# The digits for the one-hot rows in a PSUM bank taken from the scores' ring

## The chip, the cores and the metric

The kernel runs on one core of a Trainium2 chip. The metric is the device time of one execution in microseconds; lower is better. The times of three runs of the kernel before are shown, and one execution was profiled.

## The reference, cut to what matters

Two blocks of a network (a gated delta rule layer, a stick-breaking attention layer, then a layer of windowed attention and mLSTM) run on 512 tokens of width 1024. The change lies in the last part, `peer_ffn`, which picks 16 of 16384 experts for each token and head:

```python
q = (xb @ w_query).reshape(t, PEER_HEADS, 2, PEER_KEY_DIM // 2)
s = jnp.einsum('thpd,hpkd->thpk', q, sub_keys).astype(jnp.float32)
top_s, top_i = lax.top_k(s, K)
...
cand_i = (top_i[:, :, 0, :, None] * N_KEYS + top_i[:, :, 1, None, :]).reshape(t, PEER_HEADS, K * K)
best_s, best_pos = lax.top_k(cand_s, K)
idx = jnp.take_along_axis(cand_i, best_pos, axis=-1)
gate = jax.nn.softmax(best_s, axis=-1)
u = expert_down[idx]
act = jax.nn.gelu(jnp.einsum('td,thkd->thk', xb, u).astype(jnp.float32), approximate=False)
vv = expert_up[idx]
return jnp.einsum('thk,thkd->td', (gate * act).astype(xb.dtype), vv)
```

An expert's index has two digits below 128.

## The kernel before, in words

Weights are split into a high and a low part (`split`, lines 99 and 102: ACT rounds, then POOL or DVE subtracts) and each product is three matmuls (`mm3`, lines 106 to 108). In the last part (`peer`, from line 1217 on) three of the four blocks of 128 tokens are *dense*, the first is *sparse*.

- **Fills.** For each of 128 first digits j, `activations` loads 128 experts (`downr`, 512 KB), splits them (`downh`, `downl`), multiplies them with the tokens of the three dense blocks in 24 matmuls of 384 columns (tile `pj`), and writes the activations `w` to a DRAM buffer `wait`. A quarter of the subtractions runs on DVE (`SPL`), the rest on POOL. With each fill 1.25 rows of experts are fetched for the sparse block by an indirect DMA that POOL issues (`gdown`, line 1428), and DVE multiplies such a row with `xn`, which lies in PSUM (line 1438).
- **Picks.** `peer_pick` (line 1315) handles one block: scores in four groups of four heads and one half each (line 1326, PSUM tile `s`, a ring of two banks), copied by ACT to `sc` (line 1328, two buffers), scanned on DVE by `top16` (lines 1309 to 1313, five scans a head), then the candidates, the softmax and the two digits (`part`). A fill's worth of work is put between groups and heads.
- **Gate matrices.** `gate_matrix` (line 1384) makes for a dense block a 128 x 128 matrix per token: gates summed at the pair of digits. Three transposes put digit 1, digit 2 and gate of each of 128 slots on the partitions (`slots`). In steps of 8 tokens, 16 a block and 48 in all, DVE makes `one` (line 1402: does the counter 0 to 127 equal digit 1) and `hot` (line 1405: the same for digit 2), POOL multiplies `hot` by the gate (`two`, line 1407), PE multiplies `one` by `two` for each token (line 1412, tile `m`, a ring of two banks), ACT copies the result to `stage` (line 1413), and a DMA writes it to DRAM. With each step stand 1.33 fills.
- **Combine.** From about 2310 us on the second table is read, and PE sums over all experts (line 1504).

For these comparisons the counter stands in SBUF twice: `iota` (fp32, 128 columns) for `one`, `iota8` (bf16, 1024 columns, each value eight times) for `hot`, with digit 2 cast to bf16 (`slotsb`, line 1395).

PSUM has eight banks; in this part `xn` takes two, the projections' ring `pj` two, `s` two and `m` two. `SPARE_P` (line 328) names the banks that the first four query projections use: pj, pj, s, s.

The order on each engine is set by a scheduler from the written order and its own costs and waits; every engine works its instructions off in that order. So the order moves where a buffer or the kind of an operation changes.

Of the kernel before, what the change touches and what calls it, by code (L numbers as in the profile page):

```python
# [14 lines left out]
BF16 = mybir.dt.bfloat16  # L15
AF = mybir.ActivationFunctionType
ALU = mybir.AluOpType
AX = mybir.AxisListType

P = 128  # L20
# [304 lines left out]


class Gdn(Net):
    SPARE_SB, SPARE_2, SPARE_P = "pj pj l l", "pj pj l l", "pj pj s s"
    RAW, SB_, PART = 3, 3, 2
    FIRST, OFF, A0, WB, SPARE_0, SQ = (0, 8, 16), (), 12, 6, "v0", 8  # L330
    SP = 5
# [876 lines left out]
class Peer(Second):  # L1208
# [8 lines left out]
    def peer(self, x, out, dense, sparse):  # L1217
# [4 lines left out]
        nc, tc, a = self.nc, self.tc, self.a  # L1222
# [4 lines left out]
        with ExitStack() as st:  # L1227
            self.ring(2, 3, *self.S3)
            c = st.enter_context(tc.tile_pool(name="p_c", bufs=1))
            dram = st.enter_context(tc.tile_pool(name="p_dram", bufs=1, space=bass.MemoryType.DRAM))  # L1230
            sx = ExitStack()
            xn = sx.enter_context(tc.tile_pool(name="p_xn", bufs=1, space=bass.MemoryType.PSUM)).tile([P, D], F32, name="xn")
            s1 = ExitStack()
            self.psum(s1, s=2, m=2)
            keys = c.tile([P, NH, P], F32, name="keys")
            nc.sync.dma_start(keys, a["sub_keysT"])
            iota = c.tile([P, P], F32, name="iota")
# [1 line left out]
            small = c.tile([P, self.K], BF16, name="small")  # L1239
            nc.gpsimd.tensor_copy(small, iota[:, :self.K])  # L1240

            iota8 = c.tile([P, P, 8], BF16, name="iota8")
            nc.gpsimd.tensor_copy(iota8, iota.unsqueeze(2).to_broadcast([P, P, 8]))
            nH, nL = c.tile([P, KC, T], F32R, name="nH"), c.tile([P, KC, T], F32R, name="nL")
            self.gp = st.enter_context(tc.tile_pool(name="p_g", bufs=self.LAG + 2))
            qT = s1.enter_context(tc.tile_pool(name="p_q", bufs=1)).tile([P, NH, T], F32, name="pqT")
# [15 lines left out]
            wk = s1.enter_context(tc.tile_pool(name="p_wk", bufs=1))  # L1262
# [4 lines left out]
            def fill(share):  # L1267
                self.share += share
                while self.filled < min(P, int(self.share * P + 1e-6)):
                    j = self.filled  # L1270
                    self.dve += self.SPL
                    by_dve = self.dve >= 1
                    w, l = self.activations(j, N, nc.vector if by_dve else nc.gpsimd)
                    nc.sync.dma_start(wait[j], w)
                    self.due += self.RATE_1 if self.gs else 0.0
                    if by_dve:
                        self.dve -= 1
                    self.gather(min(int(self.due), sum(g[0] == "down" for g in self.gs)), None if by_dve else l, l if by_dve else None)
                    self.due -= int(self.due)
                    self.filled += 1  # L1280
            self.fill = fill
            gate, d1, d2 = self.peer_pick(wk, i0, qT, keys, small)
# [8 lines left out]
            G = []  # L1291
            for i in dense:
                gate, d1, d2 = self.peer_pick(wk, i, qT, keys, small)
                G.append(self.gate_matrix(wk, dram, i, gate, d1, d2, iota, iota8))
            fill(1.0)
            self.gather(sum(g[0] == "down" for g in self.gs))
            while self.came:
# [83 lines left out]
            part.append(o.rearrange("p h k -> p (h k)"))  # L1381
        return gate.rearrange("p h k -> p (h k)"), part[0], part[1]

    def gate_matrix(self, wk, dram, i, gate, d1, d2, iota, iota8):

        nc = self.nc
        TG = self.TG
        Gd = dram.tile([P // TG, P, P, TG], F32, name=f"G{i}")
        p = self.pg("s")
        for z, s in enumerate((d1, d2, gate)):  # L1390
            nc.tensor.transpose(p[:, z * P:(z + 1) * P], s, self.ident)
        sl = wk.tile([P, 3, P], F32, tag="slots", name=f"slots{i}", bufs=2)
        nc.scalar.copy(sl, p[:, :3 * P].rearrange("p (z t) -> p z t", z=3))
        slb = wk.tile([P, P], BF16, tag="slotsb", name=f"slotsb{i}", bufs=2)
        nc.scalar.copy(slb, p[:, P:2 * P])
        for tg in range(P // TG):
            stage = wk.tile([P, P, TG], F32, tag="stage", name=f"stage{i}_{tg}", bufs=2)
            for t8 in range(0, TG, 8):
                self.fill(self.BUILD / 16)
                tt = slice(tg * TG + t8, tg * TG + t8 + 8)  # L1400
                one = wk.tile([P, 8, P], F32, tag="one", name=f"one{i}_{tg}_{t8}", bufs=2)
                nc.vector.tensor_tensor(one, iota.unsqueeze(1).to_broadcast([P, 8, P]),
                                        sl[:, 0, tt].unsqueeze(2).to_broadcast([P, 8, P]), op=ALU.is_equal)
                hot = wk.tile([P, P, 8], BF16, tag="hot2", name=f"hot{i}_{tg}_{t8}", bufs=2)
                nc.vector.tensor_tensor(hot, iota8, slb[:, tt].unsqueeze(1).to_broadcast([P, P, 8]), op=ALU.is_equal)
                two = wk.tile([P, 8, P], F32, tag="two", name=f"two{i}_{tg}_{t8}", bufs=2)
                nc.gpsimd.tensor_tensor(two, hot.rearrange("p j t -> p t j"),
                                        sl[:, 2, tt].unsqueeze(2).to_broadcast([P, 8, P]), op=ALU.mult)
                for t4 in range(0, 8, 4):
                    pm = self.pg("m")  # L1410
                    for t in range(4):
                        nc.tensor.matmul(pm[:, t * P:(t + 1) * P], one[:, t4 + t], two[:, t4 + t], start=True, stop=True)
                    nc.scalar.copy(stage[:, :, t8 + t4:t8 + t4 + 4], pm.rearrange("p (t j) -> p j t", t=4))
            nc.sync.dma_start(Gd[tg], stage)
        return Gd
# [224 lines left out]
```

## Time and profile before

| | us |
|---|---|
| median of 3 runs (2845.3 to 2853.7) | 2853.34 |
| the profiled execution | 2852.8 |
| its span | 2851.0 |

The profile gives for each engine what it did when, and for idle time the instruction that ended it. PE is TensorE, PEld its weight loads, DVE is VectorE, ACT ScalarE, POOL GpSimd; "L1402" is line 1402 of the kernel before. A name before "<-" is written, those behind it are read. PEclk is the share of TensorE's full clock that was granted. A wait is put down to whatever ended it last.

### The profile page before, as it was taken

To read this page: it belongs to the slowest core of one execution; us is meant where nothing else is said; L and a number is where in the kernel's file an instruction comes from. 1 tells how busy PE (TensorE), PEld (TensorE's weight loads), DVE (VectorE), ACT (ScalarE), POOL (GpSimd) and SP (SyncE) were. 2 spreads that over 40 slices of the span, in tenths; PEclk is the share of its full clock that TensorE was granted. 3 is DMA by queue.
4 is the path that set the end of the run, shared out by engine and by line. 5 is a ranking of instruction groups with operands and counts; after the bars stand their busy time and mean duration, and the time that the engine had idled before them with its cause. 6 is when DMAs were issued, how large, how long until landed. Compare 5 with 4: busy or idle time off the path is not lost. (4 is left out here: it accounts for less than half of the span.)

```text
span 2851.0 us, 40457 instructions
## 1 busy us (share of the span) xinstructions
PE 2671.3 (94%) x14601; PEld 2266.0 (79%) x14601; DVE 1786.9 (63%) x3095; ACT 1210.9 (42%) x2508; POOL 1765.5 (62%) x1335
## 2 busy tenths in 40 slices
PE   6999898799998999999998989998998999999999
PEld 4877777697776877778786988898998978877777
DVE  7767664614446654122332989899899166778886
ACT  5566663636654454233333333333333333333332
POOL 4889883533333522433463468788788378888786
PEclk9999999899998999999999999999999999999999
DMA  6334331221011111221222587887987879999996
GB/s 240 108 119 125 111 113 31 76 90 60 31 39 54 56 45 60 74 69 66 69 79 89 160 296 261 284 290 256 314 277 281 276 272 344 340 333 331 333 328 227
DMA packets 206793, 499.35 MB, mean 175 GB/s; under 512 B 18304, under 2 KB 106624, under 8 KB 203520
## 3 DMA queue, kind: packets, MB, share of 16 engines
q1 hardware_dynamic: 167856, 359.19, 37.6%
q0 software_dynamic: 36864, 134.23, 13.1%
q10 hardware_dynamic: 1872, 3.33, 0.4%
q8 instruction: 115, 1.88, 0.3%
q14 instruction: 86, 0.70, 0.1%
HBM read 444.26 MB, written 52.43 MB: 174 GB/s over the span
## 5 line engine op out<-in xcount | busy, mean ns | idle before, releaser
L102 POOL TENSOR_TENSOR wl<-wr,wh 128x256 fp32r<-128x256 f32 (+2 forms) x499 | 414.8, 850 | 499.2 <-ACT wh L99 468.5
L102 POOL TENSOR_TENSOR upl<-upr,uph 128x1024 fp32r<-128x1024 f32 x128 | 312.9, 2445 | 97.0 <-ACT uph L99 96.3
L99 ACT ACTIVATE wh<-wr 128x256 fp32r<-128x256 f32 (+2 forms) x556 | 228.7, 445 | 302.6 <-PE pj L107 120.4
L106 PE MATMUL pj<-nH,downh 128*128 128x384 f32 x1024 | 354.3, 346 | 2.3 <-ACT w L1459 1.7
L108 PE MATMUL pj<-nH,downl 128*128 128x384 f32 x1024 | 349.6, 341 | 4.6 <-DVE downl L102 4.6
L107 PE MATMUL pj<-nL,downh 128*128 128x384 f32 x1024 | 348.8, 341 | 0.0
L102 POOL TENSOR_TENSOR downl<-downr,downh 128x1024 fp32r<-128x1024 f32 x96 | 243.9, 2542 | 129.3 <-ACT downh L99 126.4
L1504 PE MATMUL acc<-uph,wwh 128*128 128x512 f32 x768 | 302.7, 399 | 6.9 <-ACT wwh L99 6.9
L1504 PE MATMUL acc<-upl,wwh 128*128 128x512 f32 x768 | 305.4, 398 | 0.0
L99 ACT ACTIVATE downh<-downr 128x1024 fp32r<-128x1024 f32 x128 | 135.4, 1059 | 307.0 <-PE pj L107 163.2
L102 DVE TENSOR_TENSOR wwl<-wo,wwh 128x384 fp32r<-128x384 f32 x128 | 196.1, 1533 | 76.4 <-ACT wwh L99 70.5
L1504 PE MATMUL acc<-uph,wwl 128*128 128x512 f32 x768 | 232.4, 398 | 6.6 <-DVE wwl L102 6.5
L108 PE MATMUL pj<-hH,wl 128*128 128x512 f32 x544 | 222.8, 411 | 0.9 <-POOL wl L102 0.8
L106 PE MATMUL pj<-hH,wh 128*128 128x512 f32 x544 | 220.5, 405 | 2.1 <-ACT mo L1175 1.1
L107 PE MATMUL pj<-hL,wh 128*128 128x512 f32 x544 | 215.8, 397 | 0.0
L99 ACT ACTIVATE uph<-upr 128x1024 fp32r<-128x1024 f32 x128 | 134.8, 1053 | 174.9 <-POOL upl L102 116.1
L106 PEld LDWEIGHTS pj<-nH,downh 128*128 128x128 f32 x1024 | 193.7, 189 | 6.6 <-ACT w L1459 2.0
L108 PEld LDWEIGHTS pj<-nH,downl 128*128 128x128 f32 x1024 | 193.3, 189 | 5.3 <-DVE downl L102 4.9
L107 PEld LDWEIGHTS pj<-nL,downh 128*128 128x128 f32 x1024 | 193.6, 189 | 0.0
L1428 POOL DMA_INDIRECT gdown<-in_peer_down,idx x128 | 165.7, 1295 | 44.3 <-issue 13.7
L1504 PEld LDWEIGHTS acc<-uph,wwh 128*128 128x128 f32 x768 | 145.6, 190 | 44.6 <-ACT wwh L99 9.4
L1504 PEld LDWEIGHTS acc<-uph,wwl 128*128 128x128 f32 x768 | 144.8, 189 | 43.4 <-DVE wwl L102 8.3
(621 smaller groups left out, 6702.2 us busy)
## 6 DMA issues: line engine op xcount, KB each, us to landing
downr<-in_peer_down_j SPq DMA_DIRECT2D x128, 512.0 KB, 4.8
upr<-in_peer_up_j SPq DMA_DIRECT2D x128, 512.0 KB, 6.3
wr<-in_w_in SPq DMA_DIRECT2D x50, 512.0 KB, 4.2
ada<-in_w_ada SPq DMA_DIRECT2D x48, 512.0 KB, 3.7
wait<-w SPq DMA_DIRECT2D x128, 192.0 KB, 4.9
wo<-wait SPq DMA_DIRECT2D x128, 192.0 KB, 5.2
G<-stage SPq DMA_DIRECT2D x24, 1024.0 KB, 6.9
Gt<-G SPq DMA_DIRECT2D x48, 512.0 KB, 8.0
```

What stands on the lines that cost most here:

```text
L99: nc.scalar.activation(h, src, AF.Copy)
L102: return (eb or nc.vector).tensor_tensor(l, src, h.bitcast(F32), op=ALU.subtract)
L106: mm(out, lh, rh, start=start, stop=False)
L107: mm(out, lh, rl, start=False, stop=False)
L108: mm(out, ll, rh, start=False, stop=stop)
L1428: nc.gpsimd.indirect_dma_start(out=g, out_offset=None, in_=self.a[f"peer_{name}"], in_offset=bass.IndirectOffsetOnAxis(ap=self.idx[:, s:s ...
L1504: mm(po[z][b], lh[:, zs], rh[:, bs], start=False, stop=j == P - 1 and rh is uh and lh is l, skip_group_check=True)
```

## The change

The counter now stands once, as fp32, in a PSUM bank of its own (`k`), which DVE fills; the scores' ring has one bank instead of two. Both comparisons read the counter from there and the digits from `slots` in SBUF, `hot` as fp32 (its output stays bf16). `iota8` and `slotsb` are gone. The spare banks of the projections are now pj, pj, s, m. In the changed kernel `one` is on line 1400 and `hot` on 1403; other lines behind 1395 move up by one.

```diff
-    SPARE_SB, SPARE_2, SPARE_P = "pj pj l l", "pj pj l l", "pj pj s s"
+    SPARE_SB, SPARE_2, SPARE_P = "pj pj l l", "pj pj l l", "pj pj s m"
...
-            self.psum(s1, s=2, m=2)
+            self.psum(s1, s=1, m=2, k=1)
...
-            iota8 = c.tile([P, P, 8], BF16, name="iota8")
-            nc.gpsimd.tensor_copy(iota8, iota.unsqueeze(2).to_broadcast([P, P, 8]))
+            count = self.pg("k")[:, :P]
+            nc.vector.tensor_copy(count, iota)
...
-        slb = wk.tile([P, P], BF16, tag="slotsb", name=f"slotsb{i}", bufs=2)
-        nc.scalar.copy(slb, p[:, P:2 * P])
...
-                nc.vector.tensor_tensor(one, iota.unsqueeze(1).to_broadcast([P, 8, P]),
+                nc.vector.tensor_tensor(one, count.unsqueeze(1).to_broadcast([P, 8, P]),
                                         sl[:, 0, tt].unsqueeze(2).to_broadcast([P, 8, P]), op=ALU.is_equal)
...
-                nc.vector.tensor_tensor(hot, iota8, slb[:, tt].unsqueeze(1).to_broadcast([P, P, 8]), op=ALU.is_equal)
+                nc.vector.tensor_tensor(hot, count.unsqueeze(2).to_broadcast([P, P, 8]),
+                                        sl[:, 1, tt].unsqueeze(1).to_broadcast([P, P, 8]), op=ALU.is_equal)
```

The order of the instructions moves with it. On DVE, in the third dense block's gate matrix before (`one_2_8` is the step of tokens 8 to 15 of the third group of 16; `gdown` are rows of the sparse block, whose second row is the read of the sum):

```order
L1405 TENSOR_TENSOR hot_2_0_19456<-iota_13917,slotsb_19110 128x1024
L1438 ISA gdown_19600,act_14892<-gdown_19600,xn 128x1024
L1438 ISA act_14892 128x1
L1405 TENSOR_TENSOR hot_2_8_19511<-iota_13917,slotsb_19110 128x1024
L1402 TENSOR_TENSOR one_2_0_19454<-iota,slots_19108 128x1024
L1402 TENSOR_TENSOR one_2_8_19509<-iota,slots_19108 128x1024
L1405 TENSOR_TENSOR hot_3_0_19608<-iota_13917,slotsb_19110 128x1024
L1405 TENSOR_TENSOR hot_3_8_19663<-iota_13917,slotsb_19110 128x1024
L102 TENSOR_TENSOR downl_19774<-downr_19775,downh_19773 128x1024
```

Now, on DVE in the same place of the changed kernel (`k` is the counter in PSUM):

```order
L1400 TENSOR_TENSOR one_2_0_19448<-k_13917,slots_19104 128x1024
L1403 TENSOR_TENSOR hot_2_0_19450<-k_13917,slots_19104 128x1024
L1400 TENSOR_TENSOR one_2_8_19503<-k_13917,slots_19104 128x1024
L1403 TENSOR_TENSOR hot_2_8_19505<-k_13917,slots_19104 128x1024
L102 TENSOR_TENSOR downl_19768<-downr_19769,downh_19767 128x1024
L1437 ISA gdown_19597,act_14892<-gdown_19597,xn 128x1024
L1437 ISA act_14892 128x1
L1437 ISA gdown_19652,act_14892<-gdown_19652,xn 128x1024
L1437 ISA act_14892 128x1
L1437 ISA gdown_19709,act_14892<-gdown_19709,xn 128x1024
L1437 ISA act_14892 128x1
L1400 TENSOR_TENSOR one_3_0_19600<-k_13917,slots_19104 128x1024
```

Where two of `hot` or two of `one` stood together, and `one` behind the `hot` of a later step, each step's `one` now stands just ahead of its `hot`.

On PE, at the first pick before (`s_14331` and `s_14396` are groups two and three of scores, `pj` with `downh` a fill):

```order
L1326 MATMUL s_14266<-keys,pqT 128x128 x3
L1326 MATMUL s_14331<-keys,pqT 128x128 x4
L106 MATMUL pj_14279<-nH,downh_14273 128x384
L107 MATMUL pj_14279<-nL,downh_14273 128x384
L106 MATMUL pj_14344<-nH,downh_14338 128x384
L107 MATMUL pj_14344<-nL,downh_14338 128x384
L1326 MATMUL s_14396<-keys,pqT 128x128 x4
```

Now, on PE in the same place of the changed kernel:

```order
L1326 MATMUL s_14266<-keys,pqT 128x128 x3
L106 MATMUL pj_14279<-nH,downh_14273 128x384
L107 MATMUL pj_14279<-nL,downh_14273 128x384
L106 MATMUL pj_14344<-nH,downh_14338 128x384
L107 MATMUL pj_14344<-nL,downh_14338 128x384
L1326 MATMUL s_14331<-keys,pqT 128x128 x4
L108 MATMUL pj_14279<-nH,downl_14274 128x384
```

The second group has moved behind four matmuls of fills, and the third to 45 rows further on; at every later change of group 20 matmuls or more of fills stand between.

## Rows read from the trace of the kernel before

**Rows 1.** The page, part 1: busy us (share of span), instructions.

```profile
PE 2671.3 (94%) x14601; PEld 2266.0 (79%) x14601; DVE 1786.9 (63%) x3095; ACT 1210.9 (42%) x2508; POOL 1765.5 (62%) x1335
```

**Rows 2.** Windows of the two late stretches, as its header row names the columns.

```profile
core 0: us, PE busy (x) PEld busy (x) DVE busy (x) ACT busy (x) POOL busy (x), PEclk, DMA share, GB/s
...
1700.00:2215.00 515.00, 478.80 (x2925) 467.57 (x2924) 477.43 (x782) 191.81 (x290) 426.94 (x222) 0.98 0.82 280
...
2310.00:2851.00 541.00, 522.71 (x2209) 417.18 (x2207) 413.04 (x372) 181.46 (x245) 425.24 (x243) 0.99 0.92 318
```

**Rows 3.** Waits of PE, 1700 to 2215: us in total, times, longest us.

```profile
PE m L1412 <- DVE one L1402: 29.7, 12, 6.6
...
PE s L1391 <- DVE part L1380: 3.1, 3, 1.4
...
PE m L1412 <- POOL two L1407: 2.4, 3, 1.3
```

**Rows 4.** Lines of DVE, 1700 to 2215: count | busy us, mean ns | idle before.

```profile
L1402 DVE TENSOR_TENSOR one<-iota,slots 128x1024 f32<-128x1024 f32 x48 | 142.1, 2971 | 1.5 <-PE m L1412 1.5
...
L1405 DVE TENSOR_TENSOR hot<-iota,slotsb 128x1024 bf16<-128x1024 bf16 x48 | 69.9, 1466 | 0.0
...
L102 DVE TENSOR_TENSOR downl<-downr,downh 128x1024 fp32r<-128x1024 f32 x22 | 46.7, 2122 | 9.2 <-ACT downh L99 9.2
...
L1310 DVE FIND_INDEX8 ti<-ts,sc 128x8 uint32<-128x128 f32 x32 | 8.9, 284 | 0.0
```

**Rows 5.** Sources of three lines: ns minimum/median/maximum, first and last start.

```profile
L1402 DVE TENSOR_TENSOR one<-iota,slots x48: 1196/2044/8196, 1711.8 to 2198.6; 128x1024 f32<-128x1024 f32 x48
...
L1405 DVE TENSOR_TENSOR hot<-iota,slotsb x48: 667/681/5129, 1714.1 to 2191.7; 128x1024 bf16<-128x1024 bf16 x48
...
L1438 DVE CUSTOM_DVE_ANT_0 gdown<-gdown,xn x128: 1198/1210/1272, 1637.2 to 2221.2; 128x1024 f32<-128x1024 f32 x128
```

**Rows 6.** Timelines 2140 to 2149: start us, duration us, instruction, [idle before].

```profile
2140.27 1.21 DVE L1438 CUSTOM_DVE_ANT_0 gdown<-gdown,xn 128x1024 f32<-128x1024 f32 x1
...
2141.41 7.91 DVE L1402 TENSOR_TENSOR one<-iota,slots 128x1024 f32<-128x1024 f32 x2
...
2140.16 4.65 POOL L1407 TENSOR_TENSOR two<-hot,slots 128x1024 f32<-128x1024 bf16 x2
...
2144.76 2.34 POOL L102 TENSOR_TENSOR downl<-downr,downh 128x1024 fp32r<-128x1024 f32 x1
...
2148.33 0.98 PE L1412 MATMUL m<-two,one 128*128 128x128 f32 x3 [6.58 <-DVE one L1402]
```

**Rows 7.** Timelines, the same for 1773 to 1796, and PE at 1978.

```profile
1772.99 8.55 DVE L102 TENSOR_TENSOR downl<-downr,downh 128x1024 fp32r<-128x1024 f32 x1 [0.45 <-ACT downh L99]
...
1790.45 2.86 DVE L1402 TENSOR_TENSOR one<-iota,slots 128x1024 f32<-128x1024 f32 x1
...
1773.38 4.74 POOL L1407 TENSOR_TENSOR two<-hot,slots 128x1024 f32<-128x1024 bf16 x2
...
1778.05 2.40 POOL L102 TENSOR_TENSOR downl<-downr,downh 128x1024 fp32r<-128x1024 f32 x1
...
1793.45 1.83 PE L1412 MATMUL m<-two,one 128*128 128x128 f32 x7 [6.16 <-DVE one L1402]
...
1978.76 1.62 PE L1412 MATMUL m<-two,one 128*128 128x128 f32 x6 [4.54 <-DVE one L1402]
```

**Rows 8.** Source of line 1371, bf16 with one operand repeated, all in SBUF.

```profile
L1371 DVE TENSOR_TENSOR hot<-place,small x8: 2277/2288/2293, 1607.9 to 2081.0; 128x2048 bf16<-128x2048 bf16 x8
```

**Rows 9.** Windows, one stretch of 50 us (columns as in rows 2).

```profile
1750.00:1800.00 50.00, 40.35 (x260) 39.11 (x259) 49.09 (x49) 17.29 (x27) 41.33 (x21) 0.93 0.74 259
```

**Rows 10.** Source of line 1328 (copy that frees a score bank): who waited, us, times.

```profile
  PE s L1326: 0.8, 1
```

**Rows 11.** Timelines of POOL and DVE where the last part begins.

```profile
1513.62 1.04 POOL L1243 CAST iota<-iota 128x1024 bf16<-128x1024 f32 x1
...
1514.74 1.40 DVE L1252 SCALAR_TENSOR_TENSOR n_l<-x,cols,s 128x512 f32<-128x512 f32 x2 [4.52 <-PE s L130]
```

More of the change, by code (lines that the diff above doesn't have):

```diff
@@ L1293, in peer @@
                 gate, d1, d2 = self.peer_pick(wk, i, qT, keys, small)
-                G.append(self.gate_matrix(wk, dram, i, gate, d1, d2, iota, iota8))
+                G.append(self.gate_matrix(wk, dram, i, gate, d1, d2, count))
             fill(1.0)
@@ L1382, in peer_pick, with gate_matrix @@
         return gate.rearrange("p h k -> p (h k)"), part[0], part[1]
-    def gate_matrix(self, wk, dram, i, gate, d1, d2, iota, iota8):
+    def gate_matrix(self, wk, dram, i, gate, d1, d2, count):
         nc = self.nc
```

## The prediction

> **What bounds the kernel now.** I read the page first, then the stage by windows, the waits of TensorE (PE) there, the groups of VectorE (DVE), and last the timelines around the longest waits. The page shows PE busy for 94% of the span [rows 1], so only what makes PE wait can move the end. The edited code runs from 1700 to 2215 us, the gate stage. There PE is busy 478.8 of 515 us, and DVE, which feeds it, 477.4 of 515, more than anywhere else; GpSimd (POOL) is at 426.9 and the DMA at 0.82 of its share [rows 2]. PE's idle time has one main reason: the matmul `m` waits 29.7 us in 12 waits for `one`, the longest 6.6 us; 2.4 us more are waits for `two`, and 3.1 us the transposes' wait for `part` [rows 3]. From 2310 on the edit has no instruction; PE is busy 522.7 of 541 us there, and the DMA is at 0.92 [rows 2].
>
> Why is `one` late? It took 2971 ns in the mean, `hot` 1466 [rows 4], yet the shortest were 1196 and 667 ns and the longest 8196 and 5129 [rows 5]. Between 2141.4 and 2149.3 two of them took 7.91 us together, while POOL ran two `two` and one `downl` without a break from 2140.16 to 2147.1; then PE's `m` waited 6.58 us [rows 6]. So a DVE operation with both inputs in SBUF stands still while POOL works on SBUF. In the same stage `gdown`, also 128x1024 fp32 but with its second input (`xn`) in PSUM, took 1198 to 1272 ns in all 128 cases [rows 5], one of them beginning 0.1 us after POOL's `two` [rows 6]. After the change `one` and `hot` read exactly so: one input from PSUM, one from SBUF.
>
> **The change, part by part.**
> `one`: 48 instructions, 2.97 to 1.21 us as `gdown`: DVE gets back 48 x 1.76 = 84 us.
> `hot`: its bf16 inputs become fp32, one in PSUM. Undisturbed it takes 0.68 us now [rows 5], little over half of the fp32 operation of the same size. That goes: bf16 with one operand repeated innermost takes 2288 ns for 2048 columns [rows 8], so half of that, 1.14, for 1024, and `gdown` says 1.21. I take 1.21: against the mean of 1.47 [rows 4] DVE gets back 48 x 0.26 = 12 us, though an undisturbed `hot` loses 0.53. Together DVE falls from 477 to about 380 us in the stage.
> None of these 97 us is on the path by itself; the path gets PE's waits behind `one`. Of the 29.7 us, two waits of 6.2 and 4.5 us [rows 7] have a cause that stays: the first follows a DVE `downl` that took 8.55 us, because POOL ran from 1773.38 to 1780.45, and `downl` still has both inputs in SBUF. After it `one` took 2.86 us instead of 1.21; that and a second `hot` give back about 2 us of each. I keep 4.3 + 2.6 = 6.9 us. So the waits behind `one` fall by 29.7 - 6.9 = 22.8 us. What is late next is `two`: POOL waits for `hot`, which is 0.53 us longer where it was undisturbed; I add 1 us to its 2.4.
> The Trainium skill, "SBUF — State Buffer", section "SBUF: two separate sides", says that the port pair that DVE and GpSimd share is an exclusive lock, and that the instruction that starts first has it to its end. By that rule a `downl` that starts first is never held, the two waits would not come back, and the sum would be 7 us lower. The trace disagrees in one point: this `downl` is recorded as starting 0.39 us ahead of `two` and still ended after three POOL instructions [rows 7]. I go by the row.
> The transposes at each block's start wait 3.1 us for `part`, the end of a DVE chain that runs between `one` and `hot`; a DVE with 97 us less to do should be there earlier: -2 us, bounds 0 and -3.
> Clock: behind the long wait at 1793 the granted clock is 0.93 for 50 us, and PE idled 9.6 us of them [rows 9]: 14% of that stretch at the lower level, 1.2 GHz. The stage's mean is 0.98 [rows 2], 4% or 21 us at the lower level; at most half is lost work, 10 us, and most of it lies inside the waits counted above. I take -3, bounds 0 and -10.
> One bank of scores instead of two: a group's four score matmuls now wait until ScalarE (ACT) has copied the group before. With two banks that wait came to 0.8 us in all [rows 10]. In the new PE order 20 matmuls or more stand between groups (four at the first change of group alone); at 40.35 / 260 = 0.155 us each [rows 9] that is over 3 us for the copy to be made in. I take +1; the upper bound is a rival below.
> The start: POOL loses the cast of `iota8`, 1.04 us; DVE gains a copy of 128 columns in a gap of 4.52 us where it waits for `s` [rows 11]. If that gap were gone, the copy would cost what it takes, under 0.7 us, half of the two that took 1.40 there. The spare list changes one bank name; the fourth projection then uses an `m` bank, which nobody needs before the gate stage. ACT loses three casts and is off the path. All taken at 0, bounds -1 and +1.
> **Sum:** -22.8 + 1 - 2 - 3 + 1 = about -26 us, on the profiled execution's 2852.8 us (its span is 2851.0): 2827 us. The median of the runs, 2853.34, is 0.5 higher, which I leave aside.
> What does the time saved run into? The fills do not change, so the stage's bytes move in 490 instead of 515 us: 280 GB/s become about 295, below the 318 of the last part [rows 2]. I count nothing for that.
>
> **The rivals.**
> A. All the waits go. Without a backlog on DVE the two held `downl` are caught up before `m` needs `one`. For it: DVE would have 135 us free in the stage, and the new DVE order has `one` and `hot` evenly spaced. Then 2852.8 - 29.7 - 2.4 - 3.1 - 10 = about 2808 us.
> B. `downl` takes the place of `one`. POOL, at 83% of the stage, runs denser, and holds DVE in the 22 `downl` (2122 ns in the mean, against 1.2 undisturbed). Two of them already cost PE 10.7 us; were some four more held so, it would be 20, and the gain 5: about 2848 us, no change that shows. Against it: each `downl` has its own place behind ACT's `downh`, and DVE then has time to catch up.
> C. Slower: the single bank of scores. A pick has four groups; two banks and the two `sc` buffers let PE write all four without DVE. With one bank the last of them must wait until DVE has gone through a whole group. A head needs five scans; one is 284 ns [rows 4], so some 1.5 us a head, 6 us a group. If the two late groups of each of four picks made PE wait so, that is 8 x 6 = 48 us, and 2827 + 48 = 2875 us. It decides from 35 us on, 4.3 a group. Against it: all changes of group but the first have 20 matmuls or more between them, and the first pick has no gate stage behind it on DVE.
> D. The change doesn't do what it says: DVE is held on the one SBUF input or on its output too. Then `hot` costs 0.53 us more 48 times, 25 us on a DVE that is at 93% of the stage; half of it on PE is 2866 us, all of it 2878. The 128 `gdown` without one held speak against it.
>
> **How the numbers follow.** The measurement of this kernel can tell about 0.3% from no change, 8.6 us. Forecast 2827 us: chance 0.63. A 0.20, B 0.10, C 0.04, D 0.03. Faster by over 0.3% (below 2844.8): 0.63 + 0.20 = 0.83; within: 0.10; slower: 0.07. The range reaches down to A with a little more for the clock and the start, 2803, and up to the edge of B, 2846; C, D and most of B are left out.
>
> **What would show it.** Right: `one` and `hot` both at about 1.21 us with a maximum under 1.4; DVE near 380 us in the gate stage; PE's waits behind `one` below 8 us, and those behind `two` about 3; `downl` on DVE still over 2 us in the mean; PE's wait on `s` under 2 us; the last part as long as before, some 541 us. Wrong: `one` or `hot` with a maximum of several us (D); PE waiting for `sc` copies by tens of us (C); new waits of PE on `downl` or `two` (B); or a last part that grows by what the stage gained.

## The result and the profile after

The changed kernel took 2808.12 us (median of four runs, 2799.68 to 2821.08) against 2853.52 us for the kernel before (four runs): 0.9834 of it, with a 95% interval from 0.9804 to 0.9864, so some 45 us faster. The profiled execution took 2808.36 us. The interval excludes the forecast's 2827 us (0.991); the time is that of rival A.

Page of the changed kernel, part 1, to be read against [rows 1]:

```profile
PE 2663.2 (95%) x14601; PEld 2262.4 (81%) x14601; DVE 1698.3 (61%) x3092; ACT 1209.0 (43%) x2505; POOL 1735.8 (62%) x1338
```

Windows of the changed kernel: its gate stage, which now ends at 2185 instead of 2215 us, and the stretch behind it (columns as in [rows 2]):

```profile
1700.00:2185.00 485.00, 481.07 (x2988) 473.96 (x2987) 373.56 (x782) 194.54 (x293) 396.24 (x223) 1.00 0.86 302
2185.00:2235.00 50.00, 50.00 (x298) 50.00 (x297) 8.36 (x10) 16.04 (x24) 19.55 (x9) 1.00 0.93 292
```

PE idles 3.9 of 485 us where it idled 36.2 of 515. DVE is busy 373.6 us (before 477.4), POOL 396.2 (426.9), the granted clock is 1.00 of full speed (0.98), and the DMA moves 302 GB/s instead of 280.

Lines of DVE in the changed kernel's gate stage, which answer to [rows 4]:

```profile
L1400 DVE TENSOR_TENSOR one<-k,slots 128x1024 f32<-128x1024 f32 x48 | 58.4, 1217 | 53.9 <-PE m L1411 51.9 <-ACT slots L1393 1.9
L1403 DVE TENSOR_TENSOR hot<-k,slots 128x1024 bf16<-128x1024 f32 x48 | 58.1, 1211 | 0.0
L102 DVE TENSOR_TENSOR downl<-downr,downh 128x1024 fp32r<-128x1024 f32 x22 | 41.3, 1876 | 32.0 <-ACT downh L99 30.8 <-PE pj L108 1.2
```

The sources of `one` and `hot` there, which answer to [rows 5]:

```profile
L1400 DVE TENSOR_TENSOR one<-k,slots x48: 1196/1219/1226, 1703.4 to 2169.8; 128x1024 f32<-128x1024 f32 x48
```

```profile
L1403 DVE TENSOR_TENSOR hot<-k,slots x48: 1203/1211/1216, 1704.5 to 2170.9; 128x1024 bf16<-128x1024 f32 x48
```

No instance of either is over 1.23 us; before, the longest took 8.2 and 5.1 us. And the wait has turned round: DVE now idles 51.9 us before `one` because PE has not yet read an older step.

All waits of PE in that stage, to be read against [rows 3]:

```profile
PE s L1391 <- DVE part L1380: 3.3, 2, 2.8
PE pj L108 <- DVE downl L102: 0.7, 1, 0.7
```

Nothing is left behind `one` or `two`. Where the 44 us between the two profiled executions lie is told by the first and last start of the fills' last kind of matmul and of the last part's first kind, before and after:

```profile
L108 PE MATMUL pj<-nH,downl x1024: 332/338/687, 1570.5 to 2286.0; 128*128 128x384 f32 x171
```

```profile
L1504 PE MATMUL acc<-uph,wwh x768: 390/397/632, 2281.0 to 2845.2; 128*128 128x512 f32 x192
```

```profile
L108 PE MATMUL pj<-nH,downl x1024: 332/338/687, 1567.2 to 2240.0; 128*128 128x384 f32 x171
...
L102 DVE TENSOR_TENSOR downl<-downr,downh x32: 1202/1225/8218, 1574.6 to 2227.7; 128x1024 fp32r<-128x1024 f32 x32
```

```profile
L1503 PE MATMUL acc<-uph,wwh x768: 388/397/628, 2235.1 to 2801.3; 128*128 128x512 f32 x192
```

The fills take 1570.5 to 2286.0, 715.5 us, before and 672.8 after: -42.7. They begin 3.3 us earlier, ahead of anything that the comparisons do (the profiled executions of the experiments scatter over 1566 to 1575 us there), and the last part takes 566.2 instead of 564.2 us, +2.0. So the gain is made in the gate stage and kept.

### The profile page after: what moved, and what is told of

It reads as the page before. It is cut to its first block, busy times and chain, and to the rows that moved or that the text cites. A ratio compares the mean times of both kernels' runs of the same rounds, so it can differ in the third digit from the quotient of the medians.

```text
span 2806.6 us, 40394 instructions
## 1 busy us (share of the span) xinstructions
PE 2663.2 (95%) x14601; PEld 2262.4 (81%) x14601; DVE 1698.3 (61%) x3092; ACT 1209.0 (43%) x2505; POOL 1735.8 (62%) x1338
## 3 DMA queue, kind: packets, MB, share of 16 engines
q0 software_dynamic: 36864, 134.23, 13.4%
## 5 line engine op out<-in xcount | busy, mean ns | idle before, releaser
L102 POOL TENSOR_TENSOR downl<-downr,downh 128x1024 fp32r<-128x1024 f32 x96 | 238.1, 2482 | 134.0 <-ACT downh L99 132.9
L102 DVE TENSOR_TENSOR wwl<-wo,wwh 128x384 fp32r<-128x384 f32 x128 | 210.8, 1650 | 58.0 <-ACT wwh L99 54.6
L1503 PEld LDWEIGHTS acc<-upl,wwh 128*128 128x128 f32 x768 | 145.8, 190 | 35.0
```

The source lines that it names most:

```text
L102: return (eb or nc.vector).tensor_tensor(l, src, h.bitcast(F32), op=ALU.subtract)
L1503: mm(po[z][b], lh[:, zs], rh[:, bs], start=False, stop=j == P - 1 and rh is uh and lh is l, skip_group_check=True)
```

## The experiments

The theory: a DVE operation with two SBUF inputs stands still while POOL reads SBUF, and PE waits for what then comes late (*hold*). Its rivals: the single bank costs or matters (*bank*); the new order of the instructions made the gain (*order*); DVE's busy time counts as such (*DVE sum*). Ratios are to the kernel before, run on the same chip.

| | counter for `one` / for `hot` | median us | ratio, 95% interval |
|---|---|---|---|
| e1 | SBUF / SBUF bf16, one bank of `s` | 2851.08 | 0.9990 [0.9969, 1.0011] |
| e2 | PSUM / SBUF bf16 | 2826.74 | 0.9894 [0.9858, 0.9929] |
| e3 | SBUF / SBUF fp32 | 2874.14 | 1.0073 [1.0049, 1.0097] |
| e4 | SBUF / PSUM | 2857.28 | 1.0015 [0.9994, 1.0036] |
| e10, the change | PSUM / PSUM | 2810.87 | 0.9832 [0.9811, 0.9853] |

**e1, the bank alone.** The kernel before, with one bank of scores and a counter of tile names raised as `pg` does it (that number decides which projections' subtractions DVE makes):

```diff
-    SPARE_P = "pj pj s s"
+    SPARE_P = "pj pj s m"
...
-            self.psum(s1, s=2, m=2)
+            self.psum(s1, s=1, m=2)
...
+            self.uid += 1
```

> One bank of scores and the new spare list, but both comparisons as before (fp32 and bf16 counters in SBUF). Theory hold (DVE stands still while POOL reads SBUF): one near 3.0 us and hot near 1.5 in the mean, PE's waits behind one near 30 us, time 2853 us +- 9. Theory bank (the single bank costs): PE waits on s by 10 us or more, 2865 us or more. Theory order (the gain of the change came from the new order of the instructions): the order is nearly that of before, so 2853 too.

It is no slower and no faster. In its profile PE's waits, by who was waited for, and DVE's lines:

```profile
PE m L1413 <- DVE one L1403: 29.2, 11, 6.9
...
PE s L1327 <- ACT sc L1329: 0.7, 1, 0.7
```

```profile
L1403 DVE TENSOR_TENSOR one<-iota,slots 128x1024 f32<-128x1024 f32 x48 | 160.3, 3350 | 3.4 <-PE m L1413 3.4
...
L1406 DVE TENSOR_TENSOR hot<-iota,slotsb 128x1024 bf16<-128x1024 bf16 x48 | 70.2, 1473 | 6.9 <-POOL two L1408 6.8
```

The waits behind `one` are those of [rows 3], the wait for `sc` is 0.7 us (0.8 before). Rival C has no cost to show, and the bank by itself gains nothing. The order is less near to that of before than the expectation says: in the traces it differs on DVE and PE in many places, though it is nearer than that of the changed kernel.

**e2, `one` alone.** To e1 come the `k` bank and its copy, and `one` reads it; `hot` stays as before:

```diff
-            self.psum(s1, s=1, m=2)
+            self.psum(s1, s=1, m=2, k=1)
...
-            self.uid += 1
+            count = self.pg("k")[:, :P]
+            nc.vector.tensor_copy(count, iota)
...
-                G.append(self.gate_matrix(wk, dram, i, gate, d1, d2, iota, iota8))
+                G.append(self.gate_matrix(wk, dram, i, gate, d1, d2, count, iota8))
```

> As e1, with the counter in PSUM for one alone; the order on PE, ACT, POOL and SP is that of e1, on DVE there is one copy more. Theory hold: one 1.21 us without exception, hot still near 1.4, PE's waits behind one below 10 us, time 2815 to 2828 us. Theory order: since the order is that of e1, the time is that of e1, about 2853.

24 us less than e1, in the stated range. From 1530 us on the traces of both list the same operations in the same order on DVE, ACT, POOL and, as far as its matmuls are recorded, PE. So this gain is not one of order. Its lines of DVE and PE's wait:

```profile
L1407 DVE TENSOR_TENSOR hot<-iota,slotsb 128x1024 bf16<-128x1024 bf16 x48 | 128.9, 2695 | 7.4 <-POOL two L1409 7.3
L1404 DVE TENSOR_TENSOR one<-k,slots 128x1024 f32<-128x1024 f32 x48 | 57.6, 1211 | 5.1 <-PE m L1414 5.1
```

```profile
PE m L1414 <- DVE one L1404: 9.2, 7, 2.7
```

One part of the expectation missed: `hot` was to stay near 1.4 us and took 2.7. With `one` out of the way it is `hot` that meets POOL. The two together took 230.5 us in e1 and 186.5 here, so DVE got back 44 us, not the 103 by which `one` became shorter.

**e3 and e4, the fp32 counter in SBUF, and `hot` alone in PSUM.** e3 is the changed kernel with

```diff
-            count = self.pg("k")[:, :P]
-            nc.vector.tensor_copy(count, iota)
+            self.uid += 1
+            count = iota
```

and e4 the changed kernel where `one` reads `iota` in SBUF:

```diff
-                nc.vector.tensor_tensor(one, count.unsqueeze(1).to_broadcast([P, 8, P]),
+                nc.vector.tensor_tensor(one, iota.unsqueeze(1).to_broadcast([P, 8, P]),
```

> The changed kernel with its fp32 counter left in SBUF: hot is slow as in the change (1.2 us at best), both are held. Theory hold: one near 3 us, hot 2 us or more, time 2855 to 2885 us, slower than before. Theory DVE sum (every us of DVE counts alike): the same direction. Theory order: between 2808 and 2853.

> As e3, with the counter in PSUM for hot alone; the order is that of e3 but for one copy on DVE. Theory hold: hot 1.21 us without exception, one near 3 us, PE's waits behind one 20 to 35 us, time 2840 to 2860 us, below e3. Theory that hot's hold is what counts: near 2815.

Both came out in their ranges. e3 is 21 us slower than before, e4 17 us faster than e3 in an order that differs by the one copy. Lines of DVE in e3, then in e4, and PE's waits in e4:

```profile
L1400 DVE TENSOR_TENSOR one<-iota,slots 128x1024 f32<-128x1024 f32 x48 | 145.5, 3036 | 1.0 <-ACT slots L1393 1.0
L1403 DVE TENSOR_TENSOR hot<-iota,slots 128x1024 bf16<-128x1024 f32 x48 | 110.5, 2306 | 2.3 <-POOL two L1406 2.3
```

```profile
L1400 DVE TENSOR_TENSOR one<-iota,slots 128x1024 f32<-128x1024 f32 x48 | 148.8, 3102 | 4.0 <-ACT slots L1393 2.7 <-PE m L1411 1.2
...
L1403 DVE TENSOR_TENSOR hot<-k,slots 128x1024 bf16<-128x1024 f32 x48 | 58.2, 1213 | 17.5 <-POOL two L1406 17.5
```

```profile
PE m L1411 <- DVE one L1400: 19.6, 13, 5.5
PE m L1411 <- POOL two L1406: 13.8, 12, 2.6
```

(The profiled execution of e4 took 2869.5 us, 12 more than its median, so its waits are rather those of a long one.) From e1 to e3, where `hot` gets its slower form and is held, 23 us are lost, but the order changes too; its place in PSUM gives 17 back, at a fixed order. `hot` in PSUM pays only together with `one`: e4 to the changed kernel is 52 us by the ratios, in another order, though. At a fixed order the two places are worth 24 (e1 to e2) and 17 us (e3 to e4).

**e9, what POOL must do to hold DVE.** The kernel before, where POOL writes zeros in place of its subtraction in the fills:

```diff
+        if eb is nc.gpsimd and self.dull:
+            return eb.memset(l.bitcast(F32), 0.0)
         return (eb or nc.vector).tensor_tensor(l, src, h.bitcast(F32), op=ALU.subtract)
...
+                    self.dull = True
                     w, l = self.activations(j, N, nc.vector if by_dve else nc.gpsimd)
+                    self.dull = False
```

> The kernel before, where POOL's subtraction in the fills is replaced by a POOL write of zeros into the same tile (96 of the 128 low parts of the first table are left out, so the output is another); POOL's two still reads SBUF. Theory hold by reads (DVE's second SBUF input waits only while POOL reads SBUF): one and hot stretched only where they meet two, one below 2.2 us in the mean, and an instance that meets such a write alone stays at 1.21 us; time 2815 to 2840 us. Theory hold by any POOL work on SBUF: instances that meet a write are longer by what is left of it.

2807.32 us, 0.9826 [0.9804, 0.9848], 8 us below the stated range; `one` took 1.51 us in the mean. POOL's load fell too, and the order moved, so the time alone does not tell the two theories apart; the instances do. DVE and then POOL in the timeline of this kernel (the write of line 103, `two` of line 1411):

```profile
1752.65 3.87 DVE L1406 TENSOR_TENSOR one<-iota,slots 128x1024 f32<-128x1024 f32 x1
...
1782.16 1.21 DVE L1406 TENSOR_TENSOR one<-iota,slots 128x1024 f32<-128x1024 f32 x1
```

```profile
1753.01 2.42 POOL L1411 TENSOR_TENSOR two<-hot,slots 128x1024 f32<-128x1024 bf16 x1
1755.34 0.98 POOL L103 MEMSET downl<- 128x1024 f32 x1
...
1782.49 0.97 POOL L103 MEMSET downl<- 128x1024 f32 x1
```

The `one` at 1782.16 ran through POOL's write in 1.21 us, the one at 1752.65 waited out a `two`. Over the stage, 16 of 48 `one` met such a write and no `two`: they took 1204 to 1219 ns. (13 of them also met POOL's issue of an indirect DMA; 11 more met that alone and took 1208 to 1227 ns.) This agrees with the Trainium skill, "SBUF — State Buffer", section "Who interferes with whom": a DVE instruction with two SBUF inputs contends with a GpSimd instruction that reads SBUF, not with one that only writes it.

The same trace shows that the hold goes either way. DVE and POOL again, in the same kernel:

```profile
1765.70 1.21 DVE L1406 TENSOR_TENSOR one<-iota,slots 128x1024 f32<-128x1024 f32 x1
```

```profile
1765.93 3.25 POOL L1411 TENSOR_TENSOR two<-hot,slots 128x1024 f32<-128x1024 bf16 x1 [0.70 <-DVE hot L1409]
```

Here `one` ran in 1.21 us, and `two` took 3.25 us where it takes 2.4 undisturbed. In e9 13 `one` are recorded as starting 0.02 to 0.36 us ahead of the `two` that they meet. In nine of these pairs the `one` took 1.21 to 1.23 us and the `two` 3.1 to 3.4; in four, the one at 1752.65 among them, the `one` took 3.8 to 3.9 us and the `two` 2.4. So one of the two waits, and the recorded starts do not tell which (0.355 us ahead was not held, 0.352 us was).

**e5, DVE's spare time.** The changed kernel with the line of `hot` written twice.

> The changed kernel with every hot made twice: 48 x 1.21 = 58 us more on DVE that POOL cannot hold; DVE near 430 us in a gate stage of some 485. Theory lead (what counts is that one is ready ahead of PE; DVE time that leaves a lead costs nothing): no PE waits behind one over 3 us, 2805 to 2815 us. Theory DVE sum (DVE's time counts alike, 45 us gained for 104 us less): 58 x 45/104 = 25 us more, 2833.

2819.75 us, 0.9871 [0.9843, 0.9899]: some 11 us slower than the change by the ratios, between both theories. The intervals overlap a little (the change: 0.9811 to 0.9853 in e10), so this size is uncertain. Its PE waits:

```profile
PE pj L106 <- ACT w L1460: 6.4, 2, 5.1
...
PE m L1413 <- POOL two L1408: 3.7, 5, 1.6
```

No wait behind `one`, as the lead asks, and DVE is at 421.7 of 485 us; yet the 58 us of DVE work do not seem to have been free. PE waits 6.4 us for ACT's copy of a fill and 3.7 us for `two`. The DVE sum asked for 25 us more.

**e8 and e11, half and an eighth of the fills' subtractions on DVE.** The changed kernel with `SPL = 0.5`, and with `SPL = 0.125`, instead of 0.25.

> The changed kernel with half of the fills' subtractions on DVE instead of a quarter: 32 more downl on DVE, each with both inputs in SBUF, so exposed to holds, and 32 fewer on POOL. Theory lead: DVE has 110 us free in the stage, so 2805 to 2812 us. Rival B of the prediction (downl takes the place of one): PE waits behind one or downl by 10 us or more, 2820 or more.

> The changed kernel with an eighth of the fills' subtractions on DVE instead of a quarter: 16 held downl less on DVE, 16 more on POOL (39 us, some 25 of them in the gate stage, where POOL is busy 396 of 485 us). Theory that PE's floor is reached: 2808 +- 6 us. Theory that held downl on DVE still cost something in the changed kernel (as e8 hints): 2795 to 2803 us. Theory that POOL becomes the bound: waits of PE on downl or two, 2815 or more.

e8: 2827.59 us, 0.9894 [0.9867, 0.9921]; e11: 2829.73 us, 0.9909 [0.9892, 0.9925]. By the ratios they are 17 and 22 us slower than the change, and neither came out as the lead or PE's floor had it. Nor does either show the rival whose time it has: rival B asked for waits of 10 us or more behind `one` or `downl` in e8 (3.5 us there), and a bound by POOL for waits on `downl` or `two` in e11 (1.7 us there). PE's waits in e8 and in e11, and `downl` on DVE in e8:

```profile
PE pj L106 <- ACT w L1458: 11.4, 7, 3.9
PE m L1411 <- POOL two L1406: 4.6, 2, 2.5
...
PE pj L108 <- DVE downl L102: 3.5, 3, 2.0
```

```profile
PE s L1391 <- DVE part L1380: 13.4, 5, 4.8
PE pj L106 <- ACT w L1458: 6.8, 3, 3.6
```

```profile
L102 DVE TENSOR_TENSOR downl<-downr,downh 128x1024 fp32r<-128x1024 f32 x64 | 156.7, 2449 | 77.4 <-ACT downh L99 77.4
```

In e8 the 64 `downl` are held, 2.4 us in the mean, and the time goes in other waits, above all for the copy `w` that frees a fill's bank; `one` is waited for nowhere. In e11 the transposes' wait for `part` is 13.4 us, where the changed kernel has 5.4 over the same stretch; the one `downl` over 4 us in its gate stage starts behind the longest of these waits. The order differs from the changed kernel's in both. Which of this costs what was not followed further. A share of 0.25 is the best of the three.

**e6 and e7, a ring of one for `one`, and the bank taken from `m`.**

```diff
-                one = wk.tile([P, 8, P], F32, tag="one", name=f"one{i}_{tg}_{t8}", bufs=2)
+                one = wk.tile([P, 8, P], F32, tag="one", name=f"one{i}_{tg}_{t8}", bufs=1)
```

```diff
-    SPARE_P = "pj pj s m"
+    SPARE_P = "pj pj s s"
...
-            self.psum(s1, s=1, m=2, k=1)
+            self.psum(s1, s=2, m=1, k=1)
```

> The changed kernel with one buffer for one instead of two: DVE can make one only when PE has read the step before, so it cannot be two steps ahead. The holds of downl on DVE (up to 8 us) stay. Theory lead: PE waits behind one again, 5 to 25 us, 2815 to 2835 us. Theory that only the hold of one and hot counts: 1.2 us fit between two steps of some 7 us, so 2808 us +- 5.

> The changed kernel with the counter's bank taken from the ring of m (one bank left) and two banks of scores as before. Theory that any bank would do: 2808 +- 6 us, one and hot 1.21 us. Theory that m needs two banks (PE's second half of a step waits until ACT has copied the first, 0.6 us and some 0.3 us of delay, 48 times): 2808 + 40 = 2848 us.

e6: 2907.95 us, 1.0165 [1.0136, 1.0194], far outside both expectations; e7: 2842.63 us, 0.9948 [0.9924, 0.9973]. The first and last `m` in e6, and in e7:

```profile
L1411 PE MATMUL m<-two,one x768: 270/275/582, 1717.3 to 2323.8; 128*128 128x128 f32 x192
```

```profile
L1411 PE MATMUL m<-two,one x768: 270/275/551, 1725.4 to 2261.0; 128*128 128x128 f32 x192
```

In both the gate matrices are finished late: the last `m` starts at 2323.8 and 2261.0 us, where the changed kernel's fills end at 2240.0. The scheduler put the steps further apart, so that fills to cover them ran out: behind the last `m` both have no matmul of a fill left, the changed kernel has 315. e6 therefore does not test the lead. e7 shows that the bank had better come from the scores than from `m`: it keeps 15 of the 45 us.

**e10, the changed kernel once more,** unedited, beside other runs of the kernel before.

> The changed kernel again, on the chip of this call: 0.9834 of the kernel before, interval from 0.980 to 0.986.

0.9832 [0.9811, 0.9853]: the gain is the same.

## Why the prediction was right in kind and short in size

- *The holds.* Right. `one` and `hot` took 1.22 and 1.21 us, none over 1.23; DVE is at 373.6 us in the stage for the predicted 380. e2 and e4 show each half, e9 what in POOL's work holds. One thing is missing from the prediction: POOL is held by DVE as well, as e9 shows.
- *The step that failed* is "I keep 4.3 + 2.6 = 6.9 us" of the waits behind `one`, with the 1 us added for `two`. Nothing of either was left: 29.7 + 2.4 us and 0.9 us for `w` went to none, 33.0 us against the forecast's net 21.8. I carried the place of two held `downl` over into the new order. Of the 22 `downl` in the changed kernel's gate stage one is over 4 us (8.2, at 1882.9, where a pick runs), and DVE was ahead: it idles 51.9 us for PE. Two `one` were ready before that hold began, PE began to read the first of them during it, at 1889.1, and was busy from 1880 to 1900 without a break. Before, a hold of this length cost PE 6 us. So rival A's condition, not the likeliest case's, was met. The rule of the Trainium skill, "SBUF — State Buffer", section "SBUF: two separate sides", that the first to start keeps the lock, would by the prediction's estimate have brought the sum 7 us nearer, to 2820. The prediction set it aside because of one row; the recorded starts of e9 fit it in nine pairs of 13 and not in four.
- *Clock.* Sized at -3. PE's waits behind `downl` in the fills fell from 4.6 to 2.7 us as well. With these 1.9 and the 33.0 us counted, 42.7 - 34.9 = 7.8 us of the fills' gain have no wait beside them (the other waits changed by 0.6 us or less each). They lie in PE's busy time, which fell from 671.3 to 663.5 us over the fills, and 6.6 us of them in the matmuls `m`, the ones that stood behind the waits. Before, then after, over the fills (busy us, mean ns, idle before):

```profile
L1412 PE MATMUL m<-two,one 128*128 128x128 f32 x768 | 100.9, 288 | 33.1 <-DVE one L1402 29.7 <-POOL two L1407 2.4 <-ACT w L1459 0.9
```

```profile
L1411 PE MATMUL m<-two,one 128*128 128x128 f32 x768 | 94.3, 276 | 0.0
```

The longest `m` took 552 ns before, twice the median of 275, and 377 after. The granted clock rose from 0.98 to 1.00 of full speed over the stage, so that fewer matmuls ran at the lower level, 1.2 GHz. So the term was sized too small, and the bound of -10 holds it. No run changed the clock by itself.
- *The transposes' wait for `part`*, -2: wrong. It is 3.3 us where it was 3.1.
- *The bank of scores*, +1: e1 shows no cost, and rival C is out. *The start*, 0: -3.3 us, inside the scatter of the runs. *The last part*: 566.2 us, as long as before.
- *Rival B* (`downl` in place of `one`) did not come in the change. With twice the `downl` on DVE (e8) 17 of the 45 us are lost, but mostly in other waits than B's.
- *Rival D* is excluded by the maxima of `one` and `hot`.

What stays open: how the whole gain divides between hold and order. For 24 us, from e1 to e2, the hold of `one` is the cause, at a fixed order. The step from e2 to the changed kernel, 17 us by the ratios, moves `hot` and the order at once; that `hot` in PSUM gains at a fixed order is shown beside a held `one` alone (e3 to e4, 17 us), and the rise from a bf16 to an fp32 `hot` had to be paid. An order like the changed kernel's with the holds left in could not be tried, since the scheduler sets it from the same operands. Nor is it settled that DVE's lead alone counts and not its time as such: e5 came out between the two.

## What to carry to other kernels

Where DVE and POOL both work on SBUF, compare minimum and maximum of an operation of one shape: if some instances take several times the shortest, look at what POOL read then, and move one of DVE's two inputs to PSUM if a bank can be had. An operation that becomes slower alone can still gain, as `hot` did, if it is the one that waits. Moving only one of two neighbouring operations can pass part of the hold on to the other: with `one` moved, `hot` rose from 1.47 to 2.70 us (e2); with `hot` moved, `one` stayed as it was, 3.04 and 3.10 us (e4).

## What the runs showed of the hardware

- DVE's hold lasts through several POOL instructions in a row: 8.55 us through three [rows 7], 8.2 us in the changed kernel.
- The hold goes either way: of 13 `one` recorded as starting 0.02 to 0.36 us ahead of POOL's read (e9), four were held, and nine held POOL's `two`, which took 3.1 to 3.4 us instead of 2.4.
- A POOL write of 128x1024 fp32, 0.97 us, did not lengthen a DVE operation with two SBUF inputs: 1204 to 1219 ns in 16 cases (e9).
- POOL gained too, with one `downl` more to do: its busy time in the gate stage fell from 426.9 to 396.2 us, 24.5 of it in the 108 indirect DMAs (`gdown`) that it issues, whose mean went from 1317 to 1090 ns. Spans on POOL are rough, and why these became shorter was not tested.
